# Gated-DeltaNet and conformer block on one core: convolution taps given out step by step, two head stages moved to later steps, Y copied by ScalarE

## The chip, the cores and the metric

The kernel runs on one core of one Trainium2 chip. The metric is the device time of one execution in microseconds. Before the change three runs took 1005.62, 1006.33 and 1006.49 us (median 1006.33 us).

The engines are named as in the profile: PE is TensorE's matrix multiplication and PEld its weight load, DVE is VectorE, ACT is ScalarE, POOL is GpSimd and SP is SyncE, which issues most DMAs. Every engine works through its own list of instructions in order, and waits for semaphores of the others.

## The reference

The input x has 512 frames of 1024 channels. One layer is computed, cut here to what matters:

```python
h = rmsnorm(x, norm1_w)
q, k, v, z, b_raw, a_raw, glu, gates = split(h @ w_in)
q, k, v = silu(causal_depthwise_conv(q|k|v, dn_conv_w))     # 4 taps, 8 heads of 128
q, k = l2norm(q), l2norm(k)
o = gated_delta_rule_chunked(q, k, v, g, beta)              # chunks, triangular solve, state S
out_a = (rmsnorm(o) * silu(z)) @ dn_w_o
ga, gb = split(glu + b_glu)
c = causal_depthwise_conv(ga * sigmoid(gb), cm_dw_w)        # 31 taps, 1024 channels
out_b = silu(layernorm(c + cm_dw_b)) @ cm_w_pw2 + cm_b_pw2
x = x + (gate_a * out_a + gate_b * out_b) @ w_out           # gates: sigmoid
x = x + (silu(f_gate) * f_up) @ ffn_w_down                  # f_gate, f_up from rmsnorm(x)
return rmsnorm(x, norm_f_w)
```

## The kernel before

**Projections.** Every weight matrix is read in units of 128 rows by 1024 (512 KB). `unit` (L93, L95) issues the DMA of `raw` on SP, lets ACT round it to `whi` (float32r), and DVE subtract the two into `wlo`; each of the three tiles has three buffers. The activations are split in the same way into `hh` and `hl`. `split3` (L104) then makes three matmuls of 128x128 by 128x512 for each of eight pieces: whi with hh, whi with hl, wlo with hh. A projection `proj` so has 24 matmuls, in eight *steps* of three.

**The order of the work.** A queue of generators gives out the steps. A head is the projections of k, q, v (each behind a four-tap convolution, `conv4`, L287 on ACT and L290 on DVE, and a Silu, L293) and of z, and then eight steps of the other work (GLU units and gates): 40 steps a head (`ROUND`), 320 steps for the heads, 480 in all. At fixed steps other work is inserted between the matmuls:

- `front(h)`, after the first 18 steps of a head: PE transposes k (L303), ACT squares it (L323) and makes `kd` (L326), DVE and POOL make the norms (L328 to L332; L330 is POOL's), PE makes k times k, ACT and POOL turn it into `Un` (L339, L340), ACT takes the diagonal blocks out as `cp` and `cc` (L345, L347), and `cc` goes through DRAM by DMA into `U`. POOL then solves the 16x16 blocks: `y`, 30 small operations (L366 and L368) in a chain.
- `front2(h)`, right after z: PE transposes v (L303 again, from `vT`), ACT makes `Vp` (L376), PE multiplies k and q, DVE makes `at` (L381), and PE sums q's squares with ones (L386), into a PSUM buffer that `Vp` has read.
- `chain(h)`, from step 78 + 40h (`START`): it joins the 16x16 blocks into 64x64 blocks with small matmuls (L405 and following) and copies (`xc` L398, `Y`, `X`, `Yl`), up to L454, whose result is copied into `Y` by DVE (L455). Then follow the four chunks of the recurrence with the state S: L473, ACT's `w` (L475), L478, L485 and so on.
- the 31-tap convolutions `conv31`: 30 DVE instructions each (L534, 128x512), eight of them. All that stand ready are given out together every 40 steps.

**What sets an engine's order.** The kernel is recorded in this order, and a list scheduler then orders each engine's instructions by priority, which is by default the place where they are recorded, and by its own durations. `tc.cur_priority` can be raised: `background` adds 1600 (`OFF`) to the priority of the taps, so that they fill the gaps that other DVE work leaves. `behind` makes what is recorded inside it stand behind the instructions last marked on their engines (all of them, or one engine).

The taps' sums end in `sacc`, which `ln_mean` needs for one matmul (L552) at the end of the 480 steps.

In the rows of an order the line numbers are those of the kernel that they come from. After the change the lines of the chain behind L440 are lower by one: the copy L455 is L454, the matmul L454 is L453, L473 is L472, w's L475 is L474, L478 is L477, L485 is L484, S's L481 is L480, and the tap L534 is L533.

Of the kernel before, what the change touches and what calls it, by code (L numbers as in the profile page):

```python
# [6 lines left out]
F32 = mybir.dt.float32  # L7
# [7 lines left out]
P = 128  # L15
T = 512
NT = 4
D = 1024
KD = 8
H = 8  # L20
FF = 22
OFF = 1600
PAD = 416
START = 78
ROUND = 40
EPS = 1e-6

# [2 lines left out]
def block_kernel(ctx, tc, a):  # L30
    nc = tc.nc
    V, S, G, PE = nc.vector, nc.scalar, nc.gpsimd, nc.tensor
# [44 lines left out]
    def marked(b, kind="drain"):  # L77
        mark[b.ins.engine, kind] = b.ins
        return b

    @contextmanager
    def behind(only=None):
        with ExitStack() as st:
            for i in list(mark.values()):
                if only is None or i.engine == only:
                    st.enter_context(tc.issue_after(i))
            yield
# [29 lines left out]
    tp = keep.enter_context(tc.tile_pool(name="tp", bufs=2))  # L117
# [6 lines left out]
    cs = []  # L124
# [3 lines left out]
    with tc.tile_pool(name="st", bufs=2) as st:  # L128
# [28 lines left out]
        prio = tc.cur_priority  # L157
# [13 lines left out]
        for k in range(KD):  # L171
# [4 lines left out]
            if k % 2 == 0:  # L176
                c = slice(k * P, k * P + 256)
# [3 lines left out]
            c = slice(k * P, k * P + P)  # L181
# [4 lines left out]
        ss = st.tile([P, 2, NT], F32, name="rms_ss", bufs=1)  # L186
# [4 lines left out]
        ps = psg.tile([P, 4, P], F32, name="g")  # L191
# [8 lines left out]
        for k in range(KD):  # L200
            c = slice(k * P, k * P + P)
            split3(eps_[3], (hi[:, c], lo[:, c]), uh[:, k, :], ul[:, k, :], k == 0, k == KD - 1)
        def glu0(i):
            sg = tp.tile([P, T], F32, name="sg")
            V.tensor_tensor(out=sg, in0=eps_[2 * i], in1=rsb, op=ALU.mult)
            S.activation(sg, sg, AF.Sigmoid, bias=b_glu[:, 8 + i:9 + i])
            c = tp.tile([P, T + 30], F32, name="c", bufs=3)
            V.memset(c[:, 0:30], 0.0)
            V.tensor_tensor(out=c[:, 30:], in0=eps_[2 * i + 1], in1=rsb, op=ALU.mult)
            V.scalar_tensor_tensor(out=c[:, 30:], in0=c[:, 30:], scalar=b_glu[:, i:i + 1], in1=sg,  # L210
                                   op0=ALU.add, op1=ALU.mult)
            cs.append(c)
# [49 lines left out]
    Y = gp.tile([P, NT, P], F32, name="Y")  # L262
# [37 lines left out]
    def tok(src, pool, tag):  # L300
        ps = pool.tile([P, 4, P], F32, name=tag)
        for n in range(NT):
            PE.transpose(ps[:, n, :], src[:, n, :], ident)  # L303
        return ps
# [66 lines left out]
    def front2(kT, qT, vT, DT, ss):  # L371
        nk = ss[:, 5]
        ps = tok(vT, psg, "g")
        Vp = gp.tile([P, NT, P], F32, name="Vp", bufs=3)
        for n in range(NT):
            S.activation(Vp[:, n, :], ps[:, n, :], AF.Copy, scale=nk[:, n:n + 1])  # L376
        ps = psg.tile([P, 4, P], F32, name="g")
        for n in range(NT):
            PE.matmul(ps[:, n, :], kT[:, n, :], qT[:, n, :], start=True, stop=True)  # L379
        at = gp.tile([P, NT, P], F32, name="at", bufs=3)  # L380
        V.tensor_tensor(out=at, in0=ps, in1=DT, op=ALU.mult)  # L381
        qq = tp.tile([P, NT, P], F32, name="acc4")
        S.activation(qq, qT, AF.Square)
        ps = psg.tile([P, 4, P], F32, name="g")
        for n in range(NT):
            PE.matmul(ps[:, n, 0:1], qq[:, n, :], ones[:, 0:1], start=True, stop=True)  # L386
        S.activation(ss[:, 1], ps[:, :, 0], AF.Copy)
        return Vp, at

    def chain(h, kT, qT, ss, kd, b2, Un, Ud, Vp, at, yq, zs):  # L390
        sq = junk[:, 0:P]

        y = gp.tile([P, NT, 32], F32, name="yb")
# [9 lines left out]
        ps = psb.tile([P, 4, P], F32, name="b")  # L403
# [5 lines left out]
        ps = psb.tile([P, 4, P], F32, name="b")  # L409
# [16 lines left out]
        ps = psb.tile([P, 4, P], F32, name="b")  # L426
# [8 lines left out]
        ps = psb.tile([P, 4, P], F32, name="b")  # L435
# [1 line left out]
            PE.matmul(ps[0:64, n, 0:32], Q1[:, n, :], Yd[:, n, :], start=True, stop=True)  # L437
        yield 1
        for i in range(2):
            V.tensor_copy(out=Y[64 * i:64 * i + 32, :, 64 * i + 32:64 * i + 64],  # L440
                          in_=ps[32 * i:32 * i + 32, :, 0:32])
        for n in range(NT):
            V.transpose(out=X[32:64, n, 0:32], in_=Y[0:32, n, 32:64])
        S.copy(out=Yl[0:64], in_=Y[64:128, :, 64:128])
# [2 lines left out]
        ps = psb.tile([P, 4, P], F32, name="b")  # L447
# [4 lines left out]
        ps = psb.tile([P, 4, P], F32, name="b")  # L452
        for n in range(NT):  # L453
            PE.matmul(ps[0:64, n, 0:64], Q2[:, n, :], Yl[:, n, :], start=True, stop=True)  # L454
        V.tensor_copy(out=Y[0:64, :, 64:128], in_=ps[0:64, :, 0:64])  # L455
        yield 2


# [2 lines left out]
        for n in range(NT):  # L461
            pp = pst.tile([P, P], F32, name="sp", bufs=1)
            ps = pst.tile([P, 4, P], F32, name="st", bufs=1)
# [51 lines left out]
    def glu(i):  # L515
        pb = yield from proj(40 + i)
        sg = tp.tile([P, T], F32, name="sg")
        marked(S.activation(sg, pb, AF.Sigmoid, bias=b_glu[:, 8 + i:9 + i]))
        yield
        pa = yield from proj(32 + i)  # L520
        c = tp.tile([P, T + 30], F32, name="c", bufs=3)
        V.memset(c[:, 0:30], 0.0)
        marked(V.scalar_tensor_tensor(out=c[:, 30:], in0=pa, scalar=b_glu[:, i:i + 1], in1=sg,
                                      op0=ALU.add, op1=ALU.mult))
        cs.append(c)
        yield
# [3 lines left out]
    def conv31(i, c):  # L530
        acc = cv[i]
        S.activation(acc, c[:, 0:T], AF.Identity, scale=c31w[:, i, 0:1], bias=dw_b[:, i:i + 1])
        for k in range(1, 31):  # L533
            V.scalar_tensor_tensor(out=acc, in0=c[:, k:k + T], scalar=c31w[:, i, k:k + 1], in1=acc,  # L534
                                   op0=ALU.mult, op1=ALU.add)
        if i == 1:
            V.tensor_tensor(out=sacc, in0=cv[0], in1=cv[1], op=ALU.add)
        elif i > 1:
            V.tensor_tensor(out=sacc, in0=sacc, in1=cv[i], op=ALU.add)
# [38 lines left out]
    def step():  # L578

        while queue:  # L580
            try:
                next(queue[0])
            except StopIteration:
                queue.pop(0)
                continue
            count[0] += 1
            if count[0] % ROUND == 0:
                background()
            return True
        return False  # L590

# [9 lines left out]
    def gates(a, b):  # L601
        for i in range(a, b):
            close()
            yield from gate(i)

    def background():
        prio = tc.cur_priority
        tc.cur_priority = prio + OFF
        while len(convs) < len(cs):
            conv31(len(convs), cs[len(convs)])  # L610
            convs.append(1)
        tc.cur_priority = prio

    def decays():

        yield 2
        gps = psg.tile([P, 4, P], F32, name="g")
        fl = lambda t: t.rearrange("p n h -> p (n h)")
        for i, m in enumerate((tri, suf, ones, mid)):
            PE.matmul(gps[:, i, 0:32], m, fl(g), start=True, stop=True)  # L620
        S.activation(fl(egc), gps[:, 0, 0:32], AF.Exp)
        S.activation(fl(kdf), gps[:, 1, 0:32], AF.Exp)
        S.activation(fl(egl), gps[:, 2, 0:32], AF.Exp)
        V.tensor_scalar(out=negc, in0=egc, scalar1=-1.0, scalar2=None, op0=ALU.mult)
        V.tensor_scalar(out=fl(nmc), in0=gps[:, 3, 0:32], scalar1=-1.0, scalar2=None, op0=ALU.mult)
        mps = psg.tile([P, 4, P], F32, name="g")
        PE.matmul(mps[0:32, 0, :], fl(g), mid, start=True, stop=True)
        mr = mrt[0:32, 0:P]
        S.activation(mr, mps[0:32, 0, :], AF.Copy)
        for n in range(NT):  # L630
            nc.sync.dma_start(mrow[:, n, :], mr[n * H:(n + 1) * H])
        dts.append(decay(0))

    def head(h, done):

        k_ = yield from conv4(8 + h, "kT")
        close()
        q_ = yield from conv4(h, "qT")
        close()
        v = conv4(16 + h, "vT")  # L640
        for _ in range(2):
            next(v)
            yield
        DT = dts.pop(0)
        if h + 1 < H:
            dts.append(decay(h + 1))
        with behind():
            ss, kd, b2, Un, Ud, y = front(h, k_, DT)
        v_ = yield from v
        pz = yield from proj(24 + h)  # L650
        z_ = zall[:, h, :]
        S.activation(z_, pz, AF.Silu)
        yield
        with behind():
            Vp, at = front2(k_, q_, v_, DT, ss)
        done.append((h, k_, q_, ss, kd, b2, Un, Ud, Vp, at, y, z_))

    def others():
        for i in range(2, KD):
# [7 lines left out]
            yield  # L667


    done, ended, dts, convs, count, chains = [], [], [], [], [0], [[0, decays()]]  # L670
    rest = others()
    for h in range(H):
        queue.append(head(h, done))
# [3 lines left out]
    while step() or chains:  # L677
        if nh < H and count[0] >= START + ROUND * nh:
            chains.append([0, chain(*done[nh])])
            nh += 1  # L680
        for c in list(chains):
            if c[0] <= count[0] or not queue:
# [3 lines left out]
                    chains.remove(c)  # L686
                else:
                    c[0] = count[0] + n
    background()
    for _, sc, e in ended:  # L690
        if not sc:
            scaled(*e)
# [24 lines left out]
    for j in range(KD):  # L717
        if j == 3:
            ln_norm(vacc)
        ps = psm.tile([P, T], F32, name="mm")  # L720
# [11 lines left out]
    for j in range(KD):  # L732
        ps = psm.tile([P, T], F32, name="mm")
# [204 lines left out]
```

## Time and profile before

| | |
|---|---|
| three runs | 1005.62, 1006.33, 1006.49 us |
| profiled execution | 1009.2 us, of which 1007.4 us lie between its first and last instruction (the span) |
| granted clock of PE, mean | 0.99 |
| instructions | 13142 |
| DMA | 106.76 MB, 106 GB/s in the mean |
| busy: ACT's whi (L93) | 159.2 us in 150 |
| busy: DVE's wlo (L95), taps (L534) | 186.9 us in 150, 180.0 us in 240 |
| busy: POOL's y (L366, L368) | 101.7 us in 240 |

The times of the trace are counted from the start of the span; the profiled execution is 2.9 us above the median of the runs. In a row of the timeline stand the start, the time that the instruction took, engine, line, operation, tiles and shapes, and in brackets the idle time before it with what ended it. Successive instructions of an engine overlap a little, so the distance from start to start is often shorter than the duration. PEclk is the share of the full clock that PE was granted.

### The profile page before, as it was taken

How to read it: one execution, taken by the hardware profiler on the slowest of the kernel's cores; microseconds unless marked ns; L12 is line 12 of the kernel's file. 1: busy time of each engine (PE TensorE's matmuls, PEld its weight loads, DVE VectorE, ACT ScalarE, POOL GpSimd, SP SyncE). 2: the span in 40 equal slices, each digit the busy share in tenths (PEclk: the TensorE clock that was granted, in tenths of full speed). 3: DMA queues.
4: the chain of work that ended last, by engine and by line, in shares of the span. 5: the costliest groups of instructions: out<-in, count | busy, mean ns of one | idle time of the engine just before them, and what ended most of it. 6: DMA issues, size and time to landing. Idle time of an engine off the chain costs nothing.

```text
span 1007.4 us, 13142 instructions
## 1 busy us (share of the span) xinstructions
PE 975.0 (97%) x4844; PEld 805.0 (80%) x4844; DVE 603.5 (60%) x944; ACT 486.5 (48%) x1005; POOL 200.7 (20%) x336
## 2 busy tenths in 40 slices
PE   7998899999999999999999999999999999999997
PEld 5686687788878888888888888888888888888886
DVE  4889588898779759898486643633333333322323
ACT  6597467767878675543455323422323323212212
POOL 0323835364552433000040001100000000000201
PEclk9999799999999999999999999999999999999999
DMA  9233313223132232234844432332232232322322
GB/s 321 85 106 96 97 55 89 80 74 116 44 98 69 77 107 63 84 127 135 271 128 155 136 115 84 105 105 91 97 104 87 102 105 84 105 98 91 104 63 84
DMA packets 37200, 106.76 MB, mean 106 GB/s; under 512 B 6240, under 2 KB 8192, under 8 KB 37136
## 3 DMA queue, kind: packets, MB, share of 16 engines
q1 hardware_dynamic: 36096, 103.71, 32.1%
q0 software_dynamic: 320, 1.10, 0.4%
q10 hardware_dynamic: 720, 1.11, 0.3%
q8 instruction: 38, 0.62, 0.3%
q14 instruction: 26, 0.21, 0.1%
HBM read 99.33 MB, written 6.57 MB: 105 GB/s over the span
## 4 chain that ended last, share of the span: by engine, by line
PE 86%; ACT 4%; DVE 4%; POOL 3%; issue 2%; DMA 0%; SPq 0%; POOLq 0%; DVEq 0%; ACTq 0%
PE mm L104 60%; PE w L104 16%; DVE cv L534 2%; POOL Un L340 1%; PE g L303 1%; PE b L405 1%; ACT whi L93 1%; PE b L411 1%; PE sp L478 1%; PE g L336 1%; ACT Un L339 1%; PE st L485 1%; PE st L473 1%; PE g L379 1%; PE b L429 1%
## 5 line engine op out<-in xcount | busy, mean ns | idle before, releaser
L93 ACT ACTIVATE whi<-raw 128x1024 fp32r<-128x1024 f32 x150 | 159.2, 1061 | 361.3 <-PE mm L104 178.5
L104 PE MATMUL mm<-hh,whi 128*128 128x512 f32 x816 | 328.3, 403 | 0.0
L104 PE MATMUL mm<-hl,whi 128*128 128x512 f32 x816 | 323.2, 396 | 2.3 <-POOL hl L219 1.6
L104 PE MATMUL mm<-hh,wlo 128*128 128x512 f32 x816 | 322.3, 395 | 2.3 <-DVE wlo L95 2.3
L95 DVE TENSOR_TENSOR wlo<-raw,whi 128x1024 fp32r<-128x1024 f32 x150 | 186.9, 1246 | 189.6 <-ACT whi L93 189.2
L104 PEld LDWEIGHTS mm<-hh,wlo 128*128 128x128 f32 x816 | 154.4, 189 | 34.3 <-DVE wlo L95 2.7
L534 DVE SCALAR_TENSOR_TENSOR cv<-c,c31w,cv 128x512 f32<-128x512 f32 x240 | 180.0, 773 | 2.0
L104 PEld LDWEIGHTS mm<-hl,whi 128*128 128x128 f32 x816 | 154.5, 189 | 33.2 <-POOL hl L219 2.9
L104 PEld LDWEIGHTS mm<-hh,whi 128*128 128x128 f32 x816 | 154.6, 189 | 29.9 <-ACT hh L218 0.2
L104 PE MATMUL w<-wlo,fh 128*128 128x512 f32 (+1 forms) x176 | 67.8, 385 | 0.0
L104 PE MATMUL w<-whi,fl 128*128 128x512 f32 (+1 forms) x176 | 67.8, 385 | 0.0
L104 PE MATMUL w<-whi,fh 128*128 128x512 f32 (+1 forms) x176 | 67.8, 385 | 0.0
L870 POOL TENSOR_TENSOR o<-A,nfw 128x512 f32<-128x512 f32 x4 | 5.2, 1293 | 291.3 <-DVE A L785 291.1
L366 POOL TENSOR_TENSOR ytm<-U,y 128x60 f32<-128x60 f32 (+14 forms) x120 | 50.1, 418 | 63.7 <-DMA U<-sc 38.0
L290 DVE SCALAR_TENSOR_TENSOR acc<-mm,c4w,acc 128x511 f32<-128x511 f32 (+2 forms) x72 | 53.3, 741 | 9.9 <-ACT acc L287 9.4
L858 DVE TENSOR_TENSOR fm<-mm,fsg 128x512 f32<-128x512 f32 x21 | 14.5, 692 | 70.5 <-PE mm L104 70.5
L368 POOL TENSOR_TENSOR y<-y,ytm 128x60 f32<-128x60 f32 (+14 forms) x120 | 51.6, 430 | 9.3
L104 PE MATMUL mm<-yh,whi 128*128 128x512 f32 x128 | 50.6, 396 | 0.0
L104 PE MATMUL mm<-yh,wlo 128*128 128x512 f32 x128 | 49.8, 389 | 0.0
L104 PE MATMUL mm<-yl,whi 128*128 128x512 f32 x128 | 49.8, 389 | 0.0
L792 POOL TENSOR_SCALAR ss<-ss 128x1 f32<-128x1 f32 x17 | 5.7, 336 | 169.8 <-ACT sg L790 116.2
L104 PEld LDWEIGHTS w<-whi,fl 128*128 128x128 f32 x176 | 33.1, 188 | 6.7
(271 smaller groups left out, 1307.8 us busy)
## 6 DMA issues: line engine op xcount, KB each, us to landing
raw<-in_win_dram SPq DMA_DIRECT2D x61, 512.0 KB, 3.5
raw<-in_wgu_dram SPq DMA_DIRECT2D x44, 512.0 KB, 3.3
raw<-in_wdn_dram SPq DMA_DIRECT2D x22, 512.0 KB, 3.3
A<-in_x_dram SPq DMA_DIRECT2D x8, 512.0 KB, 6.7
U<-sc SPq DMA_DIRECT2D x64, 64.0 KB, 3.3
sgd<-sg SPq DMA_DIRECT2D x16, 256.0 KB, 2.0
raw<-in_wo_dram SPq DMA_DIRECT2D x8, 512.0 KB, 4.5
gsl<-sgd SPq DMA_DIRECT2D x16, 256.0 KB, 2.7
```

Of the source, the lines that this page charges most:

```text
L93: marked(S.activation(hi, raw, AF.Copy), "unit")
L95: marked(V.tensor_tensor(out=lo, in0=raw, in1=hi.bitcast(F32), op=ALU.subtract), "unit")
L104: marked(PE.matmul(ps, l, r, start=first and i == 0, stop=last and i == 2))
L290: marked(V.scalar_tensor_tensor(out=acc[:, s:], in0=ps[:, :T - s], scalar=c4w[:, j, k:k + 1], in1=acc[:, s:], op0=ALU.mult, op1=ALU.add))
L303: PE.transpose(ps[:, n, :], src[:, n, :], ident)
L336: PE.matmul(ps[:, n, :], kT[:, n, :], kT[:, n, :], start=True, stop=True)
L339: S.activation(Un[:, n, :], ps[:, n, :], AF.Copy, scale=nb2[:, n:n + 1])
L340: G.tensor_tensor(out=Un, in0=Un, in1=DT, op=ALU.mult)
L366: G.tensor_tensor(out=tm[:, :, 0:w], in0=U[:, k, :, k + 1:], in1=y[:, :, k:k + 1].broadcast_to([P, NT, w]), op=ALU.mult)
L368: G.tensor_tensor(out=y[:, :, k + 1:], in0=y[:, :, k + 1:], in1=tm[:, :, 0:w], op=ALU.add)
L534: V.scalar_tensor_tensor(out=acc, in0=c[:, k:k + T], scalar=c31w[:, i, k:k + 1], in1=acc, op0=ALU.mult, op1=ALU.add)
L858: V.tensor_tensor(out=fm, in0=pu, in1=sg, op=ALU.mult)
```

## The change

It has four parts.

1. **The taps.** `conv31` yields after every tap, and one generator `taps()` goes through the eight convolutions. `background` runs at each step: it adds 7 (10 after step 320) to a share and gives out one tap for each 16 of it. So 140 taps are given out in the first 320 steps and 100 in the last 160. Their priority is raised by 60 and no longer by 1600, and each is held behind the DVE instructions last marked. What is left at the end is given out there.
2. **front2** is put off by five steps: it becomes an entry of the list of chains, due at the present step plus five.
3. **The chains** start at step 84 + 40h.
4. **Y is copied by ACT**: the two copies at L440 and the one at L455. The tile `c` gets a fourth buffer.

```diff
-OFF = 1600
+OFF = 60
-START = 78
+START = 84
...
-            c = tp.tile([P, T + 30], F32, name="c", bufs=3)
+            c = tp.tile([P, T + 30], F32, name="c", bufs=4)
...
         for i in range(2):
-            V.tensor_copy(out=Y[64 * i:64 * i + 32, :, 64 * i + 32:64 * i + 64],
-                          in_=ps[32 * i:32 * i + 32, :, 0:32])
+            S.copy(out=Y[64 * i:64 * i + 32, :, 64 * i + 32:64 * i + 64], in_=ps[32 * i:32 * i + 32, :, 0:32])
...
-        V.tensor_copy(out=Y[0:64, :, 64:128], in_=ps[0:64, :, 0:64])
+        S.copy(out=Y[0:64, :, 64:128], in_=ps[0:64, :, 0:64])
...
             V.scalar_tensor_tensor(out=acc, in0=c[:, k:k + T], scalar=c31w[:, i, k:k + 1], in1=acc,
                                    op0=ALU.mult, op1=ALU.add)
+            yield
...
             count[0] += 1
-            if count[0] % ROUND == 0:
-                background()
+            background()
             return True
...
+    def taps():
+        for i in range(KD):
+            while len(cs) <= i:
+                yield
+            yield from conv31(i, cs[i])
+
     def background():
+        share[0] += 7 if count[0] <= ROUND * H else 10
         prio = tc.cur_priority
         tc.cur_priority = prio + OFF
-        while len(convs) < len(cs):
-            conv31(len(convs), cs[len(convs)])
-            convs.append(1)
+        while share[0] >= 16:
+            share[0] -= 16
+            with behind(mybir.EngineType.DVE):
+                next(conv, None)
         tc.cur_priority = prio
...
-        yield
-        with behind():
-            Vp, at = front2(k_, q_, v_, DT, ss)
-        done.append((h, k_, q_, ss, kd, b2, Un, Ud, Vp, at, y, z_))
+        def last():
+            Vp, at = front2(k_, q_, v_, DT, ss)
+            done.append((h, k_, q_, ss, kd, b2, Un, Ud, Vp, at, y, z_))
+            yield 0
+
+        chains.append([count[0] + 5, last()])
+        yield
...
-    background()
+    prio = tc.cur_priority
+    tc.cur_priority = prio + 4 * OFF
+    for _ in conv:
+        pass
+    tc.cur_priority = prio
```

Three places show what the scheduler made of it.

On POOL, around head 1's Un. DT is a decay mask of a later head, ss a norm, Un and Ud head 1's; ytm and y are head 0's solve. Before:

```order
L311 TENSOR_TENSOR DT<-DT,cst 128x512
L330 TENSOR_TENSOR ss<-ss,root_84 128x4
L340 TENSOR_TENSOR Un<-Un,DT 128x512
L366 TENSOR_TENSOR ytm<-U,y 128x4x15
L357 TENSOR_TENSOR Ud<-Un,cst 128x512
L368 TENSOR_TENSOR y<-y,ytm 128x4x15
```

The same place on POOL after the change:

```order
L311 TENSOR_TENSOR DT<-DT,cst 128x512
L330 TENSOR_TENSOR ss<-ss,root_84 128x4
L366 TENSOR_TENSOR ytm<-U,y 128x4x15
L368 TENSOR_TENSOR y<-y,ytm 128x4x15
...
L366 TENSOR_TENSOR ytm<-U,y 128x4x8
L368 TENSOR_TENSOR y<-y,ytm 128x4x8
L340 TENSOR_TENSOR Un<-Un,DT 128x512
L366 TENSOR_TENSOR ytm<-U,y 128x4x7
L357 TENSOR_TENSOR Ud<-Un,cst 128x512
```

Sixteen operations of head 0's y have moved ahead of head 1's Un.

On ACT, from the end of head 2's v projection to its vT (A is z's Silu). Before:

```order
L287 ACTIVATE acc_1489<-mm,c4w 128x512
L93 ACTIVATE whi<-raw 128x1024
L339 ACTIVATE Un<-g,ss 128x128 x4
L345 COPY cp<-Un 32x128 x4
L652 ACTIVATE A<-mm 128x512
L347 ACTIVATE cc<-cp,cst 128x64
L93 ACTIVATE whi<-raw 128x1024
L293 ACTIVATE vT<-acc_1489 128x512
```

The same place on ACT after the change:

```order
L287 ACTIVATE acc_1429<-mm,c4w 128x512
L323 ACTIVATE pa,ss<-g 128x128
L326 ACTIVATE kd<-g,sm 128x128 x3
L474 ACTIVATE w<-st,ss 128x128
L93 ACTIVATE whi<-raw 128x1024 x2
L339 ACTIVATE Un<-g,ss 128x128 x4
L293 ACT_TABLE_LOAD
L293 ACTIVATE vT<-acc_1429 128x512
L345 COPY cp<-Un 32x128 x4
```

vT has moved ahead of cp, which waits for POOL; two whi and the front's squares stand between.

On PE, in chain 3, between the last joining matmul and the recurrence's first (here with buffer numbers: mm_2714 and, after the change, mm_2834 are sums of a projection, whi and wlo its weights, b_2683 and b_2801 what becomes part of Y, st the recurrence's sums). Before:

```order
L454 MATMUL b_2683<-Yl_424,Q2_420 64x64 x4
L104 MATMUL mm_2714<-hl_91,whi_2717 128x512
L104 MATMUL mm_2714<-hh_90,wlo_2719 128x512
L104 MATMUL mm_2714<-hh_90,whi_2717 128x512
L104 MATMUL mm_2714<-hl_91,whi_2717 128x512
L104 MATMUL mm_2714<-hh_90,wlo_2719 128x512
L104 MATMUL mm_2714<-hh_90,whi_2717 128x512
L473 MATMUL st_2704<-Vp_1990,Y_418 128x128
```

The same place on PE after the change:

```order
L104 MATMUL mm_2669<-hh_90,wlo_2674 128x512
L453 MATMUL b_2801<-Yl_424,Q2_420 64x64 x4
L472 MATMUL st_2816<-Vp_1980,Y_418 128x128
L104 MATMUL mm_2834<-hh_90,whi_2837 128x512
L104 MATMUL mm_2834<-hl_91,whi_2837 128x512
L104 MATMUL mm_2884<-hh_90,whi_2887 128x512
L104 MATMUL mm_2884<-hl_91,whi_2887 128x512
L104 MATMUL mm_2834<-hh_90,wlo_2839 128x512
```

And what ACT does there, in the same names (Y_418 is what L472 reads, w_2818 comes from L472):

```order
L454 COPY Y_418<-b_2801 64x4x64
L323 ACTIVATE pa_435,ss_2696<-g_2697 128x128
L287 ACTIVATE acc4_2826<-mm_2669,c4w_78 128x512
L323 ACTIVATE pa_435,ss_2696<-g_2697 128x128
L326 ACTIVATE kd_2706<-g_2697,sm_395 128x128 x3
L474 ACTIVATE w_2818<-st_2816,ss_1756 128x128
L93 ACTIVATE whi_2837<-raw_2835 128x1024
L93 ACTIVATE whi_2887<-raw_2885 128x1024
```

Where six matmuls of a unit already under way stood between, L453, L472 and the first matmul of a new unit are now neighbours on PE, and that unit's whi stands on ACT behind the w that L472 gives. Chain 4 has the same shape, with two matmuls ahead of its first wlo and no L287 in ACT's row.

More of the change, by code (lines that the diff above doesn't have):

```diff
@@ L520, in glu @@
         pa = yield from proj(32 + i)
-        c = tp.tile([P, T + 30], F32, name="c", bufs=3)
+        c = tp.tile([P, T + 30], F32, name="c", bufs=4)
         V.memset(c[:, 0:30], 0.0)
@@ L667, in take @@
             yield
-    done, ended, dts, convs, count, chains = [], [], [], [], [0], [[0, decays()]]
+    done, ended, dts, count, share, chains = [], [], [], [0], [0], [[0, decays()]]
+    conv = taps()
     rest = others()
```

## The prediction

> **What bounds the kernel now.** I read the page first, then TensorE's waits, then windows of 25 us, and then the timelines of the engines behind each wait. The page's first part:
>
> ```profile
> PE 975.0 (97%) x4844; PEld 805.0 (80%) x4844; DVE 603.5 (60%) x944; ACT 486.5 (48%) x1005; POOL 200.7 (20%) x336
> ```
>
> TensorE (PE) is busy for 975.0 of 1007.4 us. Only its idle time and the stretches in which it runs at a lower clock can be won. The view of waits, for PE (total us, times, longest), names the idle time:
>
> ```profile
> PE g L184 <- DVE cv L166: 7.5, 1, 7.5
> PE g L303 <- ACT vT L293: 6.6, 6, 2.3
> PE b L405 <- DVE xc L398: 4.6, 1, 4.6
> PE mm L104 <- DVE wlo L95: 2.3, 1, 2.3
> PE mm L104 <- POOL hl L219: 1.6, 2, 1.3
> PE g L386 <- DVE at L381: 1.4, 1, 1.4
> ```
>
> L184 and hl belong to the start, which the change does not touch. The windows (length, busy us of PE, PEld, DVE, ACT, POOL, then PEclk, DMA share, GB/s) show where the clock was low:
>
> ```profile
> 75.00:100.00 25.00, 21.25 (x96) 17.03 (x95) 24.21 (x36) 18.90 (x45) 7.73 (x6) 0.93 0.33 97
> 100.00:125.00 25.00, 20.36 (x97) 16.77 (x96) 15.50 (x25) 11.32 (x30) 21.34 (x50) 0.80 0.31 97
> 150.00:175.00 25.00, 22.72 (x142) 18.92 (x140) 19.74 (x41) 18.21 (x48) 13.66 (x26) 0.93 0.31 95
> 550.00:575.00 25.00, 25.00 (x112) 20.71 (x111) 14.48 (x19) 6.83 (x9) 0.00 (x0) 1.00 0.51 149
> ```
>
> At 550 PE is gapless and at full clock: 112 matmuls in 25 us, 0.223 us each, and there only added waits could change anything. A low clock costs (1 - PEclk) x 25: 1.75 us, 5.0 us and 1.75 us in the first three windows. They follow the waits of 2.3 (wlo), 4.6 (xc) and 2.3 (vT of head 2).
>
> **What goes, term by term.** Ahead of the wlo wait VectorE (DVE) runs the long convolution's taps; DVE rows, then PE's:
>
> ```profile
> 68.17 10.86 DVE L534 SCALAR_TENSOR_TENSOR cv<-c,c31w,cv 128x512 f32<-128x512 f32 x10
> 86.74 1.21 DVE L95 TENSOR_TENSOR wlo<-raw,whi 128x1024 fp32r<-128x1024 f32 x1
> 88.00 0.50 PE L104 MATMUL mm<-hh,wlo 128*128 128x512 f32 x1 [2.32 <-DVE wlo L95]
> ```
>
> Nineteen taps stand between two wlo there. Afterwards at most eight do, and two wlo come earlier in the row, so I take this wait out: 2.3, with its clock 1.75. What is late next is L386 of head 0, whose 1.4 I leave.
>
> The vT wait, head 2, rows of ScalarE (ACT) and GpSimd (POOL):
>
> ```profile
> 147.64 2.47 POOL L340 TENSOR_TENSOR Un<-Un,DT 128x512 f32<-128x512 f32 x1 [1.80 <-ACT Un L339]
> 150.14 1.22 ACT L345 COPY cp<-Un 32x128 f32<-32x128 f32 x4 [2.58 <-POOL Un L340]
> 152.27 1.04 ACT L93 ACTIVATE whi<-raw 128x1024 fp32r<-128x1024 f32 x1
> 153.21 0.61 ACT L293 ACTIVATE vT<-acc 128x512 f32<-128x512 f32 x1
> ```
>
> ACT stands 2.58 us behind POOL with vT's Silu queued after it. In the new order the Silu is ahead of cp in heads 2 and 4 to 7 and only head 3 keeps the old order, with about 1.6 of the 6.6. PE reaches the transposes of vT at nearly the same count of matmuls as before, so the moved front2 alone gives no slack: 5.0 goes, and head 2's clock loss of 1.75.
>
> The first chain's wait comes from POOL (heads 0 and 1), then DVE:
>
> ```profile
> 95.88 1.45 POOL L330 TENSOR_TENSOR ss<-ss,root 128x4 f32<-128x4 f32 x1 [10.27 <-DVE ss L328]
> 98.51 1.30 POOL L340 TENSOR_TENSOR Un<-Un,DT 128x512 f32<-128x512 f32 x1 [1.18 <-ACT Un L339]
> 112.78 0.21 POOL L368 TENSOR_TENSOR y<-y,ytm 128x4 f32<-128x4 f32 x1
> 113.65 0.31 DVE L398 STREAM_TRANSPOSE xc<-yb 128x128 f32<-128x128 f32 x1 [7.84 <-ACT yb L397]
> ```
>
> Head 0's y ends at 113.0 because it starts only behind head 1's Un; xc and the chain follow. Six steps later PE asks for it 27 matmuls (6 us) after L386 of head 1 instead of 14, and half of y has run before. 4.6 and its clock 5.0 go. Removed in all: 2.3 + 1.75 + 5.0 + 1.75 + 4.6 + 5.0 = **20.4 us**.
>
> **What comes: POOL in head 1.** Sixteen of y's operations now stand between L330 and L340 of head 1. ACT's cp waits for L340, and behind cp on ACT are whi, cc and Vp; PE's L386 waits for Vp. Prices and PE's arrival:
>
> ```profile
> 102.12 0.62 POOL L366 TENSOR_TENSOR ytm<-U,y 128x56 f32<-128x56 f32 x1
> 104.05 0.61 POOL L366 TENSOR_TENSOR ytm<-U,y 128x52 f32<-128x52 f32 x1
> 104.74 0.61 POOL L368 TENSOR_TENSOR y<-y,ytm 128x52 f32<-128x52 f32 x1
> 105.43 0.27 POOL L366 TENSOR_TENSOR ytm<-U,y 128x48 f32<-128x48 f32 x1
> 105.78 0.29 POOL L368 TENSOR_TENSOR y<-y,ytm 128x48 f32<-128x48 f32 x1
> 105.13 0.68 DVE L381 TENSOR_TENSOR at<-g,DT 128x512 f32<-128x512 f32 x1
> 105.18 0.95 PE L386 MATMUL g<-cst,acc 128*128 128x1 f32 x8
> 99.84 1.22 ACT L345 COPY cp<-Un 32x128 f32<-32x128 f32 x4 [1.41 <-POOL Un L340]
> 103.82 1.13 ACT L376 ACTIVATE Vp<-g,ss 128x128 f32<-128x128 f32 x4
> ```
>
> An operation takes a start-to-start 0.69 while DVE works (104.05 to 104.74) and 0.35 once DVE has ended L381 at 105.8 (105.43 to 105.78). L330 of head 1 I leave at its time, about 95.4: its input now stands behind a conv4 tap of v, which undoes PE's earlier arrival. L330 ends at 96.8. DVE then has nine such operations queued, some 6 us, so half of the sixteen at 0.69 and half at 0.35: 8.3, to 105.1. Un 1.30, cp 1.22, whi 1.04, cc 0.3 (an estimate from cp's 0.3 each) and Vp 1.13 follow in a row; a hand-over takes 0.05 (the wlo that ends at 87.95, the matmul at 88.00), three make 0.15: 110.2. PE arrives at 105.2 + 1.1 (five matmuls of 0.223 later) - 2.3 - 1.75 + 1.5 (small waits, below) = 103.75. **Wait 6.5** (3.8 with y wholly at 0.35, 10.4 with y at 0.69 and head 2's slower Un). PE's clock after it: 1.75 as behind a wait of 2.3, or 5.0 as behind 4.6, when the stretch after held small chain matmuls. Here whole units follow, so I take 2.5.
>
> **What comes: chains 3 and 4.** PE now has L453, L472 and the next unit's first matmul side by side. L472 needs L454's copy, which is ACT's now, and on ACT the whi of that next unit stands behind w, w behind L472. Groups:
>
> ```profile
> L444 ACT COPY Yl<-Y 64x256 f32<-64x256 f32 x8 | 3.3, 407 | 0.3 <-DVE Y L440 0.2
> L455 DVE COPY Y<-b 64x256 f32<-64x256 f32 x8 | 3.3, 414 | 1.6 <-PE b L454 1.5
> L475 ACT ACTIVATE w<-st,ss 128x128 f32<-128x128 f32 x32 | 11.5, 359 | 6.7 <-PE st L473 6.3
> L93 ACT ACTIVATE whi<-raw 128x1024 fp32r<-128x1024 f32 x150 | 159.2, 1061 | 361.3 <-PE mm L104 178.5 <-PE w L104 94.1 <-issue 88.2
> L95 DVE TENSOR_TENSOR wlo<-raw,whi 128x1024 fp32r<-128x1024 f32 x150 | 186.9, 1246 | 189.6 <-ACT whi L93 189.2
> 143.56 0.29 ACT L323 ACTIVATE pa<-g 128x128 f32<-128x128 f32 x1
> 143.81 0.90 ACT L326 ACTIVATE kd<-g,sm 128x128 f32<-128x128 f32 x3
> 144.85 0.73 ACT L287 ACTIVATE acc<-mm,c4w 128x512 f32<-128x512 f32 x1
> ```
>
> The copy itself is a wash: L444, the nearest ACT copy, costs 407 ns against DVE's 414. What costs is what follows. ACT's pipelined spacing, from the starts of these last rows, is 0.25 for L323 with its read, 0.75 for kd, 0.6 for L287. Chain 4, from L453's end: hand-over 0.05, copy 0.35, L323 0.25, kd 0.75, w 0.25, whi 1.04, hand-over 0.05 = 2.74, less about 0.25 for L472's own work = 2.5; then wlo (1.25) against two matmuls (0.45) = 0.8: **3.3**. Chain 3 has L287 and one more L323 in the row (+0.85) but four matmuls ahead of its wlo, two of them behind a second whi (+0.5): **3.8**. Together 7.1 (5 if half of the ACT row is done while PE is still at L453, 9 with every piece at its full duration). Each is longer than the 2.3 that was followed by a low clock twice, 1.75 each time: 3.4 (0 to 3.5). By the Trainium skill, "TensorE: Matmul & The Clock Gate", Part 1, the clock halves after a free-running window of about 3.4 us has been idle and returns after a busy one. Taken strictly, these two waits with matmuls between their parts would rarely empty a window, and the sum would be 3.4 lower; the trace disagrees (0.93 behind 2.3), so the trace's price stands.
>
> **Small waits and hidden edits.** Head 0's vT Silu now stands behind z's Silu (about 1.1), L448 of chain 0 behind ACT's copies (0.4): 1.5 (0 to 4). The taps themselves cost nothing while DVE has time, and 60% busy leaves it:
>
> ```profile
> L534 DVE SCALAR_TENSOR_TENSOR cv<-c,c31w,cv 128x512 f32<-128x512 f32 x240 | 180.0, 773 | 2.0
> ```
>
> A hundred taps fall in the last 160 steps: per unit of 24 matmuls (5.4 us) five taps at 0.773 and one wlo at 1.25 make 5.1, so DVE just keeps up; if it did not, each missing 0.1 per unit would add 2 us over 20 units. The fourth buffer of c takes only memory.
>
> **Sum.** Added 6.5 + 2.5 + 7.1 + 3.4 + 1.5 = 21.0, removed 20.4: net +0.6 on the profiled execution's 1009.2 us (span 1007.4), so 1009.8. That execution lies 2.9 above the median of 1006.33; on the median's scale **1006.9 us**, no change. A difference of 0.2% (2 us) is about what a measurement of this kernel can tell from none.
>
> **Rivals.**
>
> *Faster: the new waits stay small.* If y runs at 0.35 throughout, head 1's wait is 3.8 with 1.75 of clock, and if chains 3 and 4 hold PE for 3 together with no lower clock and the small waits are half, 9.3 is added: net -11.1, 995.2. For it: DVE was free beside most of y (7.84 idle before L398). Against it: nine DVE operations stand just there. 0.35.
>
> *Slower: taps hold up POOL.* With all sixteen at 0.69 (11.0) and Un at the 2.47 of head 2, Vp comes 3.9 later, so the wait is 10.4 with 5.0 of clock; with 7.1, 3.4 and 1.5 behind it 27.4 is added: net +7.0, 1013.3. It decides as soon as head 1's wait and clock together pass 20.4 - 12.0 + 2 = 10.4. For it: the spread taps keep DVE busy beside y all the time, where it used to be done in one burst; and it has no idle time left there for POOL. Against it: POOL's y operations are 0.35 in the larger part of the old stretch. The Trainium skill, "GPSIMD Engine Reference", section 1, Specifications, has GpSimd's SBUF interfaces shared with VectorE, in contention with VectorE instructions of two SBUF inputs, as taps are; 0.61 against 0.27 above agrees. 0.25.
>
> *The order does not do what it says*, and both kernels wait alike elsewhere: within 2 us, 0.05, since the rows of five engines did move.
>
> **Numbers.** The forecast (net -3 to +5: 1003.3 to 1011.3) has 0.35; of it 0.08 is faster by over 0.2%, 0.17 within, 0.10 slower. With the rivals: faster 0.35 + 0.08 = 0.43, same 0.17 + 0.05 = 0.22, slower 0.25 + 0.10 = 0.35. The range reaches from the faster rival's price, less 1, to the slower one's: 994 to 1014; about 0.1 lies below, 0.1 above.
>
> **What would show it.** Right: L303's waits for vT fall to about 1.6 and L405 waits for nothing; L386 has one wait of 5 to 9 us near 104 behind Vp, with POOL's y ahead of Un; two waits of 2 to 4 us on whi or wlo beside L472 between 240 and 340 us, with a low PEclk behind them. Wrong: L386 waits under 4; no whi wait at L104; a low clock missing after 3 us of idle time; a gap at ln_mean's matmul (L552) or repeated wlo waits after step 320, which would mean that the last hundred taps do not fit.

## The result, and the profile after

The changed kernel takes 1016.87 us (median of 4 runs, 1016.43 to 1017.30) against 1006.41 us before (4 runs): a ratio of 1.0105, 95% interval 1.0087 to 1.0122. It is slower by some 10 us, where no change (1006.9) was forecast and the range ended at 1014.

PE's waits after the change (total us, times, longest):

```profile
PE g L386 <- ACT Vp L376: 8.0, 2, 6.7
PE g L184 <- DVE cv L166: 7.7, 1, 7.7
PE mm L104 <- ACT whi L93: 4.3, 2, 2.6
PE st L472 <- ACT Y L454: 2.1, 2, 1.3
PE mm L104 <- POOL hl L219: 1.7, 2, 1.3
PE st L470 <- ACT o L486: 1.5, 2, 0.8
PE g L379 <- ACT Un L339: 0.8, 1, 0.8
```

The old waits for vT, xc and the late wlo are gone. In their place stand one long wait at L386, and waits on whi and on Y in chains 3 and 4. The page's first part, and then windows at the places of these waits, with one from the stretch in which PE never waits:

```profile
PE 979.4 (96%) x4844; PEld 801.7 (79%) x4844; DVE 607.8 (60%) x920; ACT 492.0 (48%) x1030; POOL 184.3 (18%) x336
```

```profile
75.00:100.00 25.00, 22.99 (x113) 18.96 (x114) 24.03 (x33) 18.57 (x46) 7.10 (x8) 1.00 0.33 97
100.00:125.00 25.00, 18.25 (x89) 15.39 (x89) 13.18 (x20) 11.04 (x26) 17.63 (x38) 0.86 0.32 97
150.00:175.00 25.00, 24.44 (x151) 19.72 (x151) 21.07 (x43) 21.40 (x56) 13.63 (x33) 1.00 0.36 102
250.00:275.00 25.00, 21.18 (x123) 16.40 (x122) 19.17 (x38) 23.04 (x60) 7.43 (x13) 0.93 0.11 34
300.00:325.00 25.00, 21.86 (x129) 17.21 (x128) 20.33 (x35) 21.39 (x63) 5.84 (x7) 0.93 0.14 44
500.00:550.00 50.00, 50.00 (x214) 39.94 (x213) 36.48 (x38) 25.49 (x33) 12.43 (x7) 1.00 0.56 179
```

The last row is the surprise. PE is busy for all 50 us at full clock and yet does 214 matmuls. The same window before:

```profile
500.00:550.00 50.00, 50.00 (x218) 40.53 (x217) 37.30 (x41) 29.05 (x38) 12.40 (x7) 1.00 0.46 145
```

It did 218. Set side by side by the count of matmuls, the two traces drift apart steadily from 503 to 637 us, where PE multiplies yh and yl and then ma: some 0.35 us in every 60 matmuls, 3.1 us in all. From there to the end they run in parallel. Busy PE grew by 4.4 us (979.4 against 975.0) with the same 4844 matmuls.

An account of the span's 7.7 us (1015.1 against 1007.4), taken from the distance between the starts of successive PE instructions: each form's median distance is its own time, what lies above it is a gap, and inside a stretch of half clock a second such time is the clock's.

| | before | after | difference |
|---|---|---|---|
| the instructions' own time | 941.8 | 944.9 | +3.1 |
| gaps over 0.25 us | 21.6 | 24.9 | +3.3 |
| half clock before the end | 7.4 | 5.0 | -2.4 |
| distances up to 0.25 us off the median, both ways | 22.0 | 25.4 | +3.4 |
| start and rest | | | +0.3 |

Gaps and clock are what the prediction had summed (+3.2 and -2.6). The first and the fourth row it did not have.

### The profile page after: what moved, and what is told of

Read it like the earlier page. It is cut to its first block, busy times and chain, and to the rows that moved or that the text cites. A ratio compares the mean times of both kernels' runs of the same rounds, so it can differ in the third digit from the quotient of the medians.

```text
span 1015.1 us, 13130 instructions
## 1 busy us (share of the span) xinstructions
PE 979.4 (96%) x4844; PEld 801.7 (79%) x4844; DVE 607.8 (60%) x920; ACT 492.0 (48%) x1030; POOL 184.3 (18%) x336
## 4 chain that ended last, share of the span: by engine, by line
PE 85%; ACT 5%; DVE 5%; issue 3%; POOL 2%; DMA 1%; SPq 0%; POOLq 0%; DVEq 0%; ACTq 0%
PE mm L104 59%; PE w L104 16%; DVE cv L533 1%; DVE wlo L95 1%; PE g L386 1%; POOL Un L340 1%; PE st L472 1%; PE b L405 1%; PE st L470 1%; PE b L411 1%; PE st L484 1%; ACT whi L93 1%; PE b L429 1%; PE sp L466 1%; PE sp L477 0%
## 5 line engine op out<-in xcount | busy, mean ns | idle before, releaser
L95 DVE TENSOR_TENSOR wlo<-raw,whi 128x1024 fp32r<-128x1024 f32 x150 | 189.4, 1264 | 196.3 <-ACT whi L93 195.8
L533 DVE SCALAR_TENSOR_TENSOR cv<-c,c31w,cv 128x512 f32<-128x512 f32 x240 | 191.7, 804 | 3.8
L366 POOL TENSOR_TENSOR ytm<-U,y 128x60 f32<-128x60 f32 (+14 forms) x120 | 45.6, 380 | 64.3 <-DMA U<-sc 55.9
L368 POOL TENSOR_TENSOR y<-y,ytm 128x60 f32<-128x60 f32 (+14 forms) x120 | 42.8, 357 | 9.3
L104 PEld LDWEIGHTS w<-wlo,fh 128*128 128x128 f32 x176 | 33.1, 188 | 6.7
```

The costliest lines, as they stand in the source:

```text
L95: marked(V.tensor_tensor(out=lo, in0=raw, in1=hi.bitcast(F32), op=ALU.subtract), "unit")
L104: marked(PE.matmul(ps, l, r, start=first and i == 0, stop=last and i == 2))
L366: G.tensor_tensor(out=tm[:, :, 0:w], in0=U[:, k, :, k + 1:], in1=y[:, :, k:k + 1].broadcast_to([P, NT, w]), op=ALU.mult)
L368: G.tensor_tensor(out=y[:, :, k + 1:], in0=y[:, :, k + 1:], in1=tm[:, :, 0:w], op=ALU.add)
```

## The experiments

Kernels that are compared ran on one chip, beside runs of the kernel before. Its median there was 1007.5 us (e1 to e4), 1009.8 (p1 to p4), 1008.9 (q1 to q4) and 1007.8 (r1, r2), so between these groups the ratios are compared and not the times.

**e1: the operands' address.** `PAD` is the size of a filler tile that stands first in two pools, `st` and `mp`. In the built program yh starts at byte 141312 of a partition before (69 times 2048) and at 143488 after (70 times 2048, plus 128): the fourth buffer of `c` had moved it, with yl, ma, uh and ul.

```diff
-PAD = 416
+PAD = 384
```

> The changed kernel with PAD 384 for 416, so that 128 bytes fewer lie ahead of the pools st and mp. The fourth buffer of c had moved every tile behind it from a multiple of 2048 bytes to 128 bytes past one; now they are on multiples again, and no instruction moves. Theory A (the address of the matmuls' operands costs the 5 ns per matmul between 485 and 640 us): the matmuls on yh, yl, ma and cv take 227 ns again, 3.5 us go there and about 1 us in the first 50 us: 1016.9 falls to about 1012. Theory B (the taps' new place on DVE, or other traffic, slows these matmuls): no change, 1016.9, and they stay at 232 ns.

Measured: 1014.02 us, ratio 1.0067 (1.0045 to 1.0089). The matmuls of the changed kernel, and then of e1 (busy us, mean ns):

```profile
L104 PE MATMUL mm<-yh,whi 128*128 128x512 f32 x128 | 51.3, 401 | 0.0
L104 PE MATMUL mm<-yl,whi 128*128 128x512 f32 x128 | 50.5, 395 | 0.0
L104 PE MATMUL w<-whi,cv 128*128 128x512 f32 x64 | 25.4, 397 | 0.0
```

```profile
L104 PE MATMUL mm<-yh,whi 128*128 128x512 f32 x128 | 50.6, 396 | 0.0
L104 PE MATMUL mm<-yl,whi 128*128 128x512 f32 x128 | 49.8, 389 | 0.0
L104 PE MATMUL w<-whi,cv 128*128 128x512 f32 x64 | 24.9, 390 | 0.0
```

Five to seven ns of each have gone (on yh, 232 to 227 from start to start). The spans differ by 2.0 us only: 1.0 was won in the first 50 us and 3.1 between 485 and 640, but 2.2 were lost between, to the clock. e1 has 27 us at half clock against the changed kernel's 14 with the same instructions in the same order, as its window at chain 3 shows:

```profile
250.00:275.00 25.00, 21.17 (x120) 16.38 (x120) 19.16 (x38) 22.70 (x58) 7.34 (x14) 0.86 0.10 29
```

**e2: the same address in the kernel before.**

```diff
-PAD = 416
+PAD = 448
```

> The kernel before with PAD 448 for 416: its operands come to lie 128 bytes past a multiple of 2048, as after the change, and nothing else is changed. Theory A: 4 to 5 us slower, 1010.5 to 1011.5, with 232 ns per matmul on yh, yl, ma, cv. Theory B: 1006.4, unchanged, at 227 ns.

Measured: 1010.75 us, ratio 1.0035 (1.0016 to 1.0054), span 1011.1 against 1007.4, with waits and stretches of half clock of the same lengths. The matmuls on yh, and in the same way those on yl, ma and cv, are as slow as after the change:

```profile
L104 PE MATMUL mm<-yh,whi 128*128 128x512 f32 x128 | 51.3, 401 | 0.0
```

Theory A holds from both sides; B falls. The address alone costs 3.7 us of span here, a little under the 4 to 5 expected.

**p4: another distance.** `PAD = 672` in the kernel before puts the operands 1024 bytes past a multiple of 2048.

> The kernel before with PAD 672 for 416, so that the operands behind it lie 1024 bytes past a multiple of 2048. Rule J (a row of 512 float32, 2048 bytes, is read more slowly when it does not start on a multiple of 2048): 232 ns per matmul on yh, yl, ma as with a shift of 128. Rule K (only starts off a smaller grain, under 1024, cost): 227 ns as before.

Measured: 1007.21 us in one run, and the yh group is back at its old time:

```profile
L104 PE MATMUL mm<-yh,whi 128*128 128x512 f32 x128 | 50.6, 395 | 0.0
```

Rule J falls: what costs is a start off some grain of more than 128 and at most 1024 bytes. For weights it is at most 512: those cut from ma start at multiples of 512 in the kernel before, and their matmuls take 226 or 227 ns there from start to start. For the row it was not narrowed further.

**e3: one copy of Y back on DVE** (aligned as e1).

```diff
-        S.copy(out=Y[0:64, :, 64:128], in_=ps[0:64, :, 0:64])
+        V.tensor_copy(out=Y[0:64, :, 64:128], in_=ps[0:64, :, 0:64])
```

> As e1 (aligned), and the one copy of Y behind L453 back on DVE; the two others stay on ACT. Theory C (chains 3 and 4 hold PE because the copy is in ACT's row, which puts L453, L472 and a new unit side by side and that unit's whi behind w): the waits on whi and on Y go (6.4 us) and so does their half clock (3.4): about 10 us below e1. Rival D (they come from the chains' start at step 84, wherever the copy runs): the waits stay and the time is that of e1.

Measured: 1006.77 us, ratio 0.9992 (0.9977 to 1.0008), against e1's 1.0067 beside the same runs of the kernel before: 7.3 us less, where about 10 were expected. The window of chain 3:

```profile
250.00:275.00 25.00, 24.74 (x148) 19.40 (x146) 22.82 (x43) 18.76 (x57) 12.97 (x23) 1.00 0.21 64
```

And PE's waits:

```profile
PE g L386 <- ACT Vp L376: 6.7, 2, 5.4
PE st L472 <- DVE R L468: 2.1, 4, 1.2
PE sp L466 <- ACT S L480: 2.0, 4, 0.7
```

The waits on whi and Y and their half clock are gone (148 matmuls in place of 120); 4 us of new small waits in the recurrence (R, S) take part of it back. Theory C holds, rival D falls.

**e4: POOL's order in heads 0 and 1 by hand** (aligned, copies on ACT). Head 0's first ten y operations go ahead of head 1's L330, the others behind its Un.

```diff
+        with tc.issue_after(first_y):
             G.tensor_tensor(out=nk, in0=kk, in1=root4, op=ALU.pow)
...
-        G.tensor_tensor(out=Un, in0=Un, in1=DT, op=ALU.mult)
+        un = G.tensor_tensor(out=Un, in0=Un, in1=DT, op=ALU.mult)
+        with tc.issue_after(un.ins):
+            rest_of_y_of_head_0()
```

> As e1 (aligned, copies on ACT), and POOL's order in heads 0 and 1 set by hand: ten of head 0's y operations ahead of L330 of head 1, then Un of head 1, then the other twenty. Theory E (sixteen y operations ahead of head 1's Un hold PE at L386): L386 waits 1 to 2 us for Vp in place of 6.7, no half clock follows, and the end of y may cost L405 of chain 0 up to 2: 5 to 7.5 us below e1. Rival F (ACT's whi and Vp would be late anyway, POOL is only the last named): less than 2 us below e1.

Measured: 1012.89 us, ratio 1.0053 (1.0037 to 1.0070), 1.1 us under e1, a difference that their intervals do not tell from none.

```profile
PE b L422 <- POOL ytm L375: 3.0, 1, 3.0
...
PE g L403 <- ACT Vp L393: 1.3, 1, 1.3
```

(L403 is L386 and L422 is L405 in this kernel's lines. L422 reads xc, which ends 0.15 us before it starts, and not the `ytm` that is named.) The wait at L386 falls from 5.4 to nothing beyond the 1.3 of head 0, as E says, but 3.0 of it come back at chain 0, with half clock behind them. Neither E's time nor F's mechanism was right: the wait had moved.

**The parts alone, from the kernel before.** p1 takes the taps (and `c`, aligned), p2 `START = 84` and the later front2, p3 the three copies.

> The kernel before with the taps given out one by one alone (c with four buffers, PAD 384 so that the operands stay on multiples of 2048 bytes); front2, the chains' start and the copies of Y are as before. Theory G (the spread taps alone put y ahead of head 1's Un, and the vT waits go only with the later front2): L386 waits 5 to 7 us for Vp, the wlo wait of 2.3 goes, L303's waits for vT stay at 5 to 7, and the chain-0 wait on xc shrinks, since PE is late already: within 5 us of before, 1002 to 1008. Rival H (the spread taps remove the vT waits by leaving POOL its port): vT waits under 3, and 998 to 1003.

> The kernel before with front2 five steps later and the chains from step 84 alone; taps in bursts, Y copied by DVE, c with three buffers. Theory G: vT stands ahead of cp on ACT in heads 2 to 7, so L303's waits for vT go (6.6 and 1.75 of clock), Un stays ahead of y in head 1, and chain 0 is asked for 18 matmuls later, so its wait of 4.6 and the 5.0 of clock go too; the wlo wait of 2.3 stays. 12 to 18 us faster than before: 990 to 995. Rival H (the taps in bursts make these waits, not the steps): within 3 us of before.

> The kernel before with the three copies of Y on ACT alone. Theory C' (the copies cost only where they put a new unit's whi behind w; here three matmuls or more stay between the last joining matmul and the recurrence, and eight to sixteen before the next new unit): within 2 us of before, and no wait of PE on whi. Rival I (ACT's copies delay every chain): L472's waits on Y appear, 4 us or more slower.

Measured against 1009.78 us: p1 1001.83 us, ratio 0.9917 (0.9902 to 0.9932); p2 1003.97, 0.9942 (0.9929 to 0.9954); p3 1004.56, 0.9947 (0.9933 to 0.9961). Each alone is *faster*. The waits of p1, then of p2:

```profile
PE g L386 <- ACT acc L383: 5.9, 1, 5.9
PE g L303 <- ACT vT L293: 3.0, 4, 1.6
```

```profile
PE b L405 <- DVE xc L398: 2.7, 1, 2.7
PE mm L104 <- DVE wlo L95: 2.3, 1, 2.3
PE st L471 <- ACT o L487: 1.9, 1, 1.9
PE sp L478 <- ACT w L475: 1.6, 2, 1.2
```

The long wait of head 1 comes with the taps alone (`acc`, which is named in p1, stands behind cp and Vp on ACT there, and cp waits for POOL's Un as in the changed kernel). The vT waits go wholly with the later steps, and half of them with the taps (3.0, between G and H). p1 gains 8 us, more than the 5 that G allowed. p2 won less than the 12 expected: 2.7 stay at L405 and 4.6 us of small waits (o, w, S) come up in the recurrence. p3 won 5 us where at most 2 were expected: its vT waits are 4.5 in place of 6.6, and it has 10 us at half clock where the kernel before's profile has 17.

**Pairs.** q1 is taps and later steps, q2 later steps and copies, q3 is q1 with e4's order on POOL.

> Two parts together: the taps one by one with the later front2 and chains; all three copies of Y on DVE; operands on multiples of 2048 bytes. Theory L (only all three parts together put L453, L472 and a new unit side by side; the order of this pair has four to six matmuls there in each chain): no wait of PE on whi and no low clock after 240 us; the L386 wait of 5 to 7 stays; vT and xc waits are gone: 3 to 9 us faster than before. Rival M (the later steps and the spread taps already clash without the copies): a loss against before, or waits of 4 us in chains 3 and 4.

> Two parts together: front2 and the chains later, the three copies of Y on ACT; taps in bursts, c with three buffers. Theory L: no wait on whi beside L472 (six matmuls stand there in chains 3 and 4), Un ahead of y in head 1, vT waits gone: 5 to 10 us faster than before, since each of the two alone was 5 to 6 faster, and part of both was the clock. Rival M' (late chains with ACT's copies are what clashes): the waits on whi and Y of 4 to 6 us appear.

> As q1 (taps and later steps, copies on DVE) with POOL's order of heads 0 and 1 set as in e4. If the wait at L386 is all that the y operations cost: 4 to 6 us below q1 less what L405 waits for y (3.0 in e4 with its half clock): 0 to 4 below q1. If the wait only moves: that of q1.

Measured: q1 1004.75 us, 0.9960 (0.9946 to 0.9974); q2 1005.45, 0.9973 (0.9961 to 0.9985); q3 1003.32, 0.9941 (0.9924 to 0.9958). No pair has a wait on whi in its list, and no half clock after 125 us. Theory L holds for the pairs tried (taps with copies was not run): in chains 3 and 4 of the parts and pairs at least three matmuls stand between L453 and L472, and only in the three parts together are L453, L472 and a new unit's first matmul neighbours. q2's gain of 3.4 us by the medians is below the 5 to 10 expected. q3 moves the wait from L386 to chain 0, 2.9 us, like e4.

**q4, r1, r2: can the wait of head 1 be won, or only moved?** All three are p1 with e4's order. q4 also has chain 0 alone eight steps later. It does not compute the layer and is no version to use; that chain 0 then reads blocks of Y which chain 1 has begun to overwrite is the likely reason, read from the code and not shown. r1 and r2 start all chains from step 82 and 84.

> The taps one by one alone (as p1), POOL's order of heads 0 and 1 set as in e4, and chain 0 alone eight steps later, so that it does not ask for y at once. Theory E: neither L386 (5.9 in p1) nor L405 waits over 1.5, no half clock near 105: 5 to 8 us below p1, 13 to 17 below before, and so below both kernels. Rival F: ACT or DVE is late at the same place anyway, within 3 of p1.

> The taps one by one alone (p1), POOL's order of heads 0 and 1 by hand as in e4, and all chains from step 82 (front2 not moved), so that every chain keeps its distance of 40 steps to the next and the reference is computed. PE asks for y 25 matmuls (5.6 us) after L386 of head 1; in e4 y ended 6 us after L386 and xc 3.7 later. If what was won at L386 can be kept: L405 waits 2 to 4, and the time is 2 to 5 us below p1. If it only moves: that of p1, within 2.

> As r1 with the chains from step 84: PE asks for y 31 matmuls (6.9 us) after L386. If the step of chain 0 sets what is left: L405 waits 1 to 3 us less than in r1. If DVE's row (wlo and c ahead of xc) sets it: the same wait as in r1.

Measured: q4 999.32 us, 0.9908 (0.9890 to 0.9926); r1 1003.30, 0.9946 (0.9919 to 0.9973); r2 998.04, 0.9905 (0.9882 to 0.9928). p1 had 0.9917, so none of the three is clear of it: q4, with no wait over 1.8 us at these places, was expected 5 to 8 us below p1, and r1 2 to 5. DVE's row in r2:

```profile
111.38 1.23 DVE L95 TENSOR_TENSOR wlo<-raw,whi 128x1024 fp32r<-128x1024 f32 x1 [6.27 <-ACT whi L93]
112.52 0.75 DVE L539 SCALAR_TENSOR_TENSOR c<-mm,vec,sg 128x512 f32<-128x512 f32 x1
113.18 0.30 DVE L415 STREAM_TRANSPOSE xc<-yb 128x128 f32<-128x128 f32 x1
```

In both, xc (L415 here) starts 10.2 us after L386, behind a wlo that waits for whi and behind c; six more matmuls ahead of the chain take 1.4 off PE's wait (3.8 in r1, 2.4 in r2), which is their own time. So xc's place in DVE's row sets when chain 0 can go on, and the step sets how much of that PE waits. r2's shorter wait has no half clock behind it and r1's has 10 us of it, which makes most of the 5 us between them in these executions. p1 and r2 are faster than both kernels (about 0.991 of the time before), and p1 needs nothing by hand.

## Why the prediction was wrong

**Right: what goes.** The waits on vT (6.6, forecast to keep 1.6), xc and the late wlo are gone, and the windows at 75 and 150 us are at 1.00.

**Right: POOL in head 1**, forecast 6.5 and measured 6.7. The changed kernel's POOL, ACT and PE:

```profile
97.11 1.01 POOL L330 TENSOR_TENSOR ss<-ss,root 128x4 f32<-128x4 f32 x1 [12.05 <-DVE ss L328]
101.08 0.60 POOL L368 TENSOR_TENSOR y<-y,ytm 128x52 f32<-128x52 f32 x1
105.27 0.25 POOL L368 TENSOR_TENSOR y<-y,ytm 128x36 f32<-128x36 f32 x1
106.13 1.26 POOL L340 TENSOR_TENSOR Un<-Un,DT 128x512 f32<-128x512 f32 x1
107.42 1.22 ACT L345 COPY cp<-Un 32x128 f32<-32x128 f32 x4 [6.20 <-POOL Un L340]
109.87 1.12 ACT L376 ACTIVATE Vp<-g,ss 128x128 f32<-128x128 f32 x4
111.04 1.87 PE L386 MATMUL g<-cst,acc 128*128 128x1 f32 x8 [6.75 <-ACT Vp L376]
```

About half of the sixteen operations took 0.6 and the others 0.25, as assumed, and PE resumed at 111.0 (forecast 110.2). The wait came out closer than its parts, which is in part luck: L330 ended 1.3 us later than assumed, and PE arrived 0.5 later. The slower rival, all sixteen slow, did not happen. The kernel is slow for another reason than that rival's.

**Right: chains 3 and 4**, forecast 7.1 and measured 4.3 on whi and 2.1 on Y. Chain 3 in the changed kernel, PE's rows and ACT's between them:

```profile
266.65 0.49 PE L472 MATMUL st<-Vp,Y 128*128 128x128 f32 x2 [1.26 <-ACT Y L454]
267.58 0.87 ACT L326 ACTIVATE kd<-g,sm 128x128 f32<-128x128 f32 x3
268.33 0.38 ACT L474 ACTIVATE w<-st,ss 128x128 f32<-128x128 f32 x1
268.58 2.02 ACT L93 ACTIVATE whi<-raw 128x1024 fp32r<-128x1024 f32 x2
269.71 0.80 PE L104 MATMUL mm<-hh,whi 128*128 128x512 f32 x1 [2.56 <-ACT whi L93]
```

1.26 and 2.56 make 3.8, the forecast. What it did not say, and e3, the parts and the pairs show, is that no part alone makes these waits, nor either of the pairs tried.

**Wrong: "The fourth buffer of c takes only memory."** This is the step that failed by a mechanism: the sum had no term for a matmul's own time. It takes the matmul operands off their addresses, and e2, where nothing else differs, prices that at 3.7 us of span (ratio 1.0035). The clue stood in the code: two filler tiles of 416 words, in the two pools behind `tp`, serve no other end than the place of what follows them.

**Wrong in size: the small waits**, forecast 1.5. L470 and L379 wait 2.3, and the distances within a quarter of a us of their medians add 3.4 net, of which the address has a part: e2 has 0.9 of it. Where the steps are late the recurrence waits on o, S, w and R in pieces of 0.2 to 1.9 us, in p2, q1, q2 and e3 too. For the short distances the traces point elsewhere: a projection's matmul that follows a small matmul and precedes another of its own kind takes 0.315 us from start to start in place of 0.227, and PE's order has 145 of these after the change and 115 before, 2.6 us more. The sum put nothing down for them, and they could have been counted in the order; that they are the whole of the rest is not shown.

**Wrong: the step from the profiled execution to the median.** The 2.9 us by which that one execution of the kernel before lay above its median were taken off the forecast for the changed kernel. Its profiled execution lies at its median (1016.88 and 1016.87). The 2.9 were most likely that execution's clock: among the kernel before's runs beside the experiments, thirty had the same mean clock of 0.990 and took 1008.2 to 1010.6 us, and twelve had 0.994 or 0.995 and took 1003.8 to 1006.9. Of the 10.0 us between forecast and result, 7.1 are in the span (7.7 against 0.6) and 2.9 are this.

**Right in sum, but for a wrong reason: the clock.** It was charged at 1.75 us or more behind every wait of 2.3 us or more. The wlo wait of 2.3, at the same place in the same order, is followed by a low clock in the kernel before and in e2 (0.93), but not in p4, nor with the same wait in p2, p3 and q2. The window at 75 us in p3:

```profile
75.00:100.00 25.00, 21.21 (x102) 17.23 (x101) 25.00 (x37) 19.57 (x48) 8.61 (x7) 1.00 0.33 97
```

In every trace with more than one stretch of half clock, all begin on one grid of 3.41 us (in the kernel before at 89.2, 113.1 and 154.1 us, 7 and 12 steps apart), and before the end of the span each is one, two or three steps long. Laid on that grid, carried back where its stretches come later, 2.2 us of this wait fell into one step in the kernel before and 1.9 in e2, and half clock followed. In p3 it was 1.8, in p2 and q2 1.5 and in p4 1.3, and none followed. So what a wait of this length costs depends on where it falls on the grid. The bound is not a general one: in e1 a step at 76.4 us with 1.3 us idle, among small matmuls, was followed too.

The Trainium skill's free-running window ("TensorE: Matmul & The Clock Gate", Part 1), which the prediction set aside, agrees with the grid better than a fixed price does. Its idle window of about 3.4 us is not met by a wait of 2.3, yet some of these were followed by half clock. A forecast does not know where a wait will fall, so for it this is a chance and not a sum. That the sum came out (-2.4 against -2.6) is luck: e1, with the same order, lost 9.9 us to the clock by the account above where the changed kernel lost 5.0.

## What to carry to other kernels

Before adding a buffer, look at what lies behind it in memory: here 128 bytes cost 2 to 4% in each of 576 matmuls, with no idle time and no wait to show it, and only the count of matmuls in a window of full PE gave it away. Parts that each gain can lose together, where each part takes a distance that the other needed; check pairs of neighbours in the orders of the *whole* change, and run the parts alone. A wait that an order removes should be followed to the next engine's row: it was ACT's, then POOL's, then DVE's.

## What the hardware showed unexpectedly

- A matmul of 128x512 float32r starts 232 ns after the one before, not 227, when its operands lie 128 bytes past a multiple of 2048; 1024 bytes past costs nothing. In the 384 matmuls on yh and yl only the row of 512 had moved, and whi and wlo are the weights. In the 192 on ma and cv whi and wlo are the row, and of all operands only ma, a weight, had moved; those on ma take 232 and 233 ns in place of 227, and those on cv, beside ma's loads, 235 in place of 226. So a moved row and moved weights both cost. Whether their own start counts, or its distance from the tiles that stayed, was not tried.
- The same instructions in the same order had 14 us at half clock in one execution and 27 us in another (the changed kernel and e1).
- Seven of POOL's y operations in a row took 0.60 to 0.75 us each after the change, beside DVE's taps, and the next ones some 0.25 once DVE had stopped.
